# Four gated tiles and the residual rows transposed by VectorE in blocks, with the tap spectrum and the decay issued later

## The chip, the cores and the metric

One core of a Trainium2 chip runs the whole kernel. Its engines are TensorE (PE; its weight loads are listed as PEld), VectorE (DVE), ScalarE (ACT), GpSimd (POOL) and SyncE (SP); 16 DMA engines move data between device memory and the on-chip buffer. The metric is the device time of one execution in microseconds.

## The reference

Two post-norm layers over 256 latent tokens with 256 context tokens ahead of them, width 1024, in fp32. Layer 0 mixes tokens with a conformer convolution, layer 1 with a bidirectional mLSTM; each is followed by a squared-ReLU MLP.

```python
# each sub-layer: x <- LN(ALPHA*x + gate * F(x*(1+scale)+shift))
def conformer_conv(u, rows, w_pw1, b_pw1, w_dw, b_dw, ln_g, ln_b, w_pw2, b_pw2):
    a = u @ w_pw1 + b_pw1
    a = a[..., :CONV_DIM] * jax.nn.sigmoid(a[..., CONV_DIM:])
    ...
        a = dwconv(a, w_dw)                                   # 31 taps
    ...
    a = jax.nn.silu(layer_norm(a + b_dw, ln_g, ln_b))
    return a @ w_pw2 + b_pw2

def mlstm_chunk_scan(q, k, v, i_pre, f_pre, state):
    ...
    lf = jax.nn.log_sigmoid(f_pre)
    ...
        bcum = jnp.cumsum(lfc, axis=-1)
        dlog = bcum[..., :, None] - bcum[..., None, :] + ic[..., None, :]
    ...
def mlstm_features(...):
    up = u @ w_up
    ...
    q, k, v = xc @ w_q, xc @ w_k, xm @ w_v
    gates = jnp.concatenate([q, k, v], axis=-1) @ w_gate + b_gate
    o = jax.nn.sigmoid(xm @ w_o + b_o)
```

## The kernel before

**Products.** Activations lie with channels on the 128 partitions and the 512 tokens along them. An fp32 product is made of three matmuls (lines 182, 185, 186, or 213 to 215): each operand is split in a high and a low part, and low times low is dropped. For weights, SP loads a block of 1 MB into a buffer `raw` (three buffers, line 145); ACT copies each half to its high part `wh` (line 151), and DVE subtracts that from the source to get the low part `wl` (line 152). Four pairs of such parts exist. A split stands in the order of ACT and DVE among all else that these engines do.

**Order.** A tile scheduler puts the instructions of each engine in a fixed order and adds the waits; `issue_after` holds an instruction back behind another one. Each queue runs in order, so an instruction that waits holds up all that stand behind it on its engine. The DMAs have eight completion lanes in turn; a DMA can also wait for the one that used its lane before.

**Start.** The first weights are those of the adaLN unit (`ada_w`, line 344), with `start0` and its fellows loading a block of x, a block of pw1 and a block of ada_w for each of eight steps. The small parameter columns `vecs` (408 floats for each partition) come in two DMAs: 64 columns first, and the rest after the second step's loads (lines 117 and 657).

**The convolution.** `pw1_epi` gates the outputs of the first product: for tile f, ACT takes the sigmoid of the gate (line 791) and DVE multiplies (line 795). The gated tile `a` has 128 channels and 512 tokens. The convolution is done in the frequency domain over windows of tokens, so the tiles must stand with tokens on the partitions, in A (4 blocks of 128 tokens x 1024 channels). `turn` does that with four transposes on TensorE (line 806) into a PSUM bank `ln`, which ACT copies to A (line 807). Tiles 0 to 2 are kept in `turns` and turned when the next output of the product is at hand. There are two `ln` banks. `taps(h)` makes half of the spectrum of the taps: two matmuls from a table `tab` of cosines and sines (line 741), which DVE makes in some 25 small steps, each result copied by ACT to `Hc` and `Hs` (line 742). The forward products of A stand at line 830.

**The residual rows.** At the head of layer 1, x of the latent tokens, scaled for the residual, is written as token rows to device memory (`r_dr`): 16 transposes on TensorE (line 1202) with ACT's copies (line 1204) into R, one write on ACT's queue, and a load back into R (`res`) in the attention stage, where it is needed at the end of that layer. v is turned differently, by DVE in blocks of 32x32 (line 1261): the blocks' places are then put right by the write to device memory.

**The gates and the attention stage.** `gate_o` makes the output gate's product and yields after every few matmuls; other work, written as generators, is stepped forward in these places. One of them, `decay`, makes the log forget gates `lf` on ACT and DVE (ending with line 1421 on DVE), their running sums with triangular matrices on TensorE (line 1435), the columns `acol`, their transposes (line 1443) and the row maxima. A `yield` in it sets how many steps of `gate_o` go by.

Of the kernel before, what the change touches and what calls it, by code (L numbers as in the profile page):

```python
# [71 lines left out]
def hybrid_kernel(ctx: ExitStack, tc: tile.TileContext, xT, vecs_d, wdw_d, ada0_w, ada_w, wg_d, pw1a, pw1, pw2, w1_0, w2_0,  # L72
# [583 lines left out]
    start0(1)  # L656
    nc.sync.dma_start(vecs[:, NV0:], vecs_d[:, NV0:])
    for f in range(DT):
# [121 lines left out]


    A = padp.tile([P, 4, D], F32, name="A")
# [18 lines left out]
    turns = []  # L801

# [108 lines left out]
    def pw1_next(m, ps):  # L911
# [12 lines left out]
        pw1_epi(m + KO0, ps)  # L924
        if m in (1, 2):
            taps(m - 1)
        if m in (4, 6):
# [262 lines left out]

    def rows_tile():
        return xp.tile([P, 2, D], F32, tag="res", name=nm("res"), bufs=1)

    r_dr = dp.tile([P, 2, D], F32, name="r_dr")
    R = rows_tile()
    for f in range(0, DT, 2):
        t, tr = tmp("S"), psum("cv")
        for i in range(2):
            nc.scalar.activation(t[:, i * C:(i + 1) * C], x[f + i][:, HI], AF.Identity, scale=al[:, 0, f + i:f + i + 1],
                                 bias=al[:, 1, f + i:f + i + 1])  # L1200
            for tt in range(2):
                nc.tensor.transpose(tr[:, tt * C + i * P:tt * C + (i + 1) * P],
                                    t[:, i * C + tt * P:i * C + (tt + 1) * P], ident)
# [188 lines left out]
    def decay(_):  # L1392
# [36 lines left out]
        yield  # L1429
        yield  # L1430
        bps = psum("ln")
        for d, cum in ((0, upper), (1, lower)):
# [533 lines left out]
def _layout(np, i):  # L1966
    g = {k: np.asarray(v) for k, v in i.items()}
    a, turned = {}, _turned(np)
    a["xT"] = np.concatenate([g["ctx"][0], g["x"][0]], axis=0).T
    vec = {  # L1970
        "c_ctx": _cols(g["c_ctx"]), "c": _cols(g["c"][0]),
        "b_pw1": _cols(g["conv_b_pw1"][0]),
        "cln_g": _cols(g["conv_ln_g"][0]), "cln_b": _cols(g["conv_ln_b"][0]),
# [16 lines left out]
    a["wg_d"] = wg.reshape(3, ET, P, 16).transpose(0, 2, 1, 3).reshape(3, P, 256)  # L1990
    pw1 = g["conv_w_pw1"][0].reshape(D, 2, DT, P).transpose(0, 2, 1, 3)[:, :, ::-1, :].reshape(D, 2 * D)
    a["pw1a"] = pw1[:, :512].reshape(DT, P, 512)
# [14 lines left out]
    a["w2_1"] = g["mlp_w2"][1].reshape(16, 2, P, D).transpose(0, 2, 1, 3).reshape(16, P, 2048)  # L2007
    ab = g["ada_b"][1].reshape(6, D)
    a["rows_d"] = np.stack([ab[2], ab[5], g["ln1_g"][1], g["ln1_b"][1], g["ln2_g"][1], g["ln2_b"][1]])
# [24 lines left out]
```

## Time and profile before

| | |
|---|---|
| three runs | 1668.18, 1663.39, 1667.71 us; median 1667.71 |
| the profiled execution | 1665.14 us, its span 1663.4 us, granted TensorE clock 0.999 |
| busy | PE 1648.7, DVE 1038.1, ACT 734.6 us |
| DMA | 303.70 MB, 183 GB/s on average |

How to read the rows: engine, source line, operation, the tile written, an arrow, and the tiles read. In a row of the chain or the timeline the first two numbers are the start from the span's beginning and the length; what stands in square brackets is the idle time of the engine before the instruction and what ended it. "xN" counts instructions that were merged. A row of the waits gives the total, the number of times and the longest, in us. A row by stretches gives, after the stretch and its length, the busy time and number of instructions of PE, PEld, DVE, ACT and POOL, then the granted clock, the share of the DMA engines' time and GB/s.

### The profile page before, as it was taken

The page shows a single profiled execution, that of the slowest core. Times are in us where ns is not written, and L with a number is a line of the kernel's source. Part 1 is how long each engine was busy: PE and PEld are TensorE (multiplying, and loading weights), DVE is VectorE, ACT ScalarE, POOL GpSimd, SP SyncE. Part 2 cuts the span into 40 slices and gives each one's busy share as a digit, 9 for nine tenths or more (in the row PEclk, how much of TensorE's full clock was granted, in tenths as well). Part 3 has the DMA queues.
Part 4 walks back from the last instruction along what each step waited for, and adds up shares of the span by engine and source line. Part 5 has one row for each costly group of instructions (what it writes and reads, how often), then busy time and mean ns, then how long its engine had stood idle before and what let it go on. Part 6 is the DMA issues. An engine that isn't in the chain of part 4 may idle for free.

```text
span 1663.4 us, 22731 instructions
## 1 busy us (share of the span) xinstructions
PE 1648.7 (99%) x8856; PEld 1357.6 (82%) x8856; DVE 1038.1 (62%) x1863; ACT 734.6 (44%) x1182; POOL 14.4 (1%) x64
## 2 busy tenths in 40 slices
PE   9999999999999999999999999999999999999998
PEld 6665898888888998877787899888877888878886
DVE  6554895666535765762354753553489876776677
ACT  4313573232324476652233533442477654555453
POOL 0000000000000000000000000000000000000001
PEclk9999999999999999999999999999999999999999
DMA  9555223534324065557774852554465555675552
GB/s 353 208 210 214 92 75 111 167 123 148 136 101 152 4 228 194 184 196 266 278 259 146 302 179 79 179 194 144 148 240 197 203 215 203 250 284 183 178 194 85
DMA packets 74331, 303.70 MB, mean 183 GB/s; under 512 B 7694, under 2 KB 23858, under 8 KB 44144
## 3 DMA queue, kind: packets, MB, share of 16 engines
q1 hardware_dynamic: 56368, 286.49, 49.1%
q10 hardware_dynamic: 17856, 15.77, 2.8%
q8 instruction: 69, 1.13, 0.3%
q14 instruction: 38, 0.31, 0.1%
HBM read 285.42 MB, written 16.81 MB: 182 GB/s over the span
## 4 chain that ended last, share of the span: by engine, by line
PE 95%; DVE 2%; DMA 1%; ACT 1%; issue 0%; SPq 0%; DVEq 0%; ACTq 0%
PE mm L182 18%; PE mm L185 17%; PE mm L186 17%; PE mm L197 7%; PE mm L198 4%; PE mm L215 3%; PE mm L213 3%; PE mm L214 3%; PE cv L213 2%; PE cv L215 2%; PE cv L214 2%; PE fl L344 1%; PE ln L182 1%; PE cv L860 1%; PE ln L214 1%; PE ln L185 1%
## 5 line engine op out<-in xcount | busy, mean ns | idle before, releaser
L152 DVE TENSOR_TENSOR wl<-raw,wh 128x1024 fp32r<-128x1024 f32 x344 | 418.7, 1221 | 245.5 <-ACT wh L151 233.4
L151 ACT CAST wh<-raw 128x1024 fp32r<-128x1024 f32 x344 | 358.6, 1051 | 469.3 <-PE mm L185 244.4
L185 PE MATMUL mm<-u,wh 128*128 128x512 f32 (+1 forms) x808 | 291.5, 361 | 0.2 <-DVE u L604 0.2
L182 PE MATMUL mm<-u,wh 128*128 128x512 f32 (+1 forms) x680 | 243.8, 359 | 0.0
L186 PE MATMUL mm<-u,wl 128*128 128x512 f32 (+1 forms) x680 | 241.3, 355 | 0.0
L185 PEld LDWEIGHTS mm<-u,wh 128*128 128x128 f32 x808 | 152.7, 189 | 23.2 <-issue 1.0
L182 PEld LDWEIGHTS mm<-u,wh 128*128 128x128 f32 x680 | 128.4, 189 | 24.4 <-issue 6.3
L186 PEld LDWEIGHTS mm<-u,wl 128*128 128x128 f32 x680 | 128.5, 189 | 17.8
L213 PE MATMUL mm<-wh,xl 128*128 128x512 f32 x256 | 101.0, 395 | 0.7 <-DVE og L1588 0.7
L182 PE MATMUL mm<-xm,wh 128*128 128x512 f32 x256 | 101.0, 394 | 0.0
L215 PE MATMUL mm<-wl,xl 128*128 128x512 f32 x256 | 100.0, 393 | 0.0
L214 PE MATMUL mm<-wh,xl 128*128 128x512 f32 x256 | 99.9, 390 | 0.0
L186 PE MATMUL mm<-xm,wl 128*128 128x512 f32 x256 | 99.7, 389 | 0.0
L182 PE MATMUL mm<-hid,wh 128*128 128x512 f32 (+1 forms) x256 | 93.3, 364 | 0.0
L186 PE MATMUL mm<-hid,wl 128*128 128x512 f32 (+1 forms) x256 | 92.8, 363 | 0.0
L185 PE MATMUL mm<-hid,wh 128*128 128x512 f32 (+1 forms) x256 | 92.8, 363 | 0.0
L197 PE MATMUL mm<-x,wh 128*128 128x512 f32 x232 | 81.1, 398 | 0.0
L185 PE MATMUL mm<-qq,wh 128*128 128x272 f32 x256 | 73.9, 289 | 0.0
L182 PE MATMUL mm<-qq,wh 128*128 128x272 f32 x256 | 73.5, 288 | 0.0
L186 PE MATMUL mm<-qq,wl 128*128 128x272 f32 x256 | 73.5, 288 | 0.0
L197 PE MATMUL mm<-u,wh 128*128 128x512 f32 x192 | 68.6, 399 | 0.0
L1099 DVE SCALAR_TENSOR_TENSOR x<-mm,ada,x 128x256 f32<-128x256 f32 x64 | 28.5, 479 | 63.4 <-PE mm L186 63.4
(537 smaller groups left out, 3249.4 us busy)
## 6 DMA issues: line engine op xcount, KB each, us to landing
raw<-w SPq DMA_DIRECT2D x64, 1024.0 KB, 4.9
raw<-wo SPq DMA_DIRECT2D x32, 1024.0 KB, 4.9
raw<-ada_w SPq DMA_DIRECT2D x22, 1024.0 KB, 7.0
ar<-ada_w SPq DMA_DIRECT2D x80, 256.0 KB, 3.9
raw<-wv SPq DMA_DIRECT2D x16, 1024.0 KB, 8.0
raw<-wqT SPq DMA_DIRECT2D x16, 1024.0 KB, 5.7
raw<-wq SPq DMA_DIRECT2D x16, 1024.0 KB, 5.8
raw<-wk SPq DMA_DIRECT2D x16, 1024.0 KB, 5.2
```

The source lines that it names most:

```text
L151: c = nc.scalar.copy(hi, src)
L152: lastsub[0] = nc.vector.tensor_tensor(lo, src, hi.bitcast(F32), op=ALU.subtract).ins
L182: a = nc.tensor.matmul(ps, wh, xh, start=start, stop=False)
L185: nc.tensor.matmul(ps, wh, xl, start=False, stop=False)
L186: lastmm[0] = nc.tensor.matmul(ps, wl, xh, start=False, stop=stop).ins
L197: todo = [lambda s_, e_: nc.tensor.matmul(ps, wh, r[0], start=s_, stop=e_), lambda s_, e_: nc.tensor.matmul(ps[:, :n], wl, r[0][:, :n], st ...
L198: lambda s_, e_: nc.tensor.matmul(ps[:, :n], wl, r[0][:, :n], start=s_, stop=e_)]
L213: nc.tensor.matmul(ps, xh, wh, start=start, stop=False)
L214: nc.tensor.matmul(ps, xl, wh, start=False, stop=False)
L215: nc.tensor.matmul(ps, xh, wl, start=False, stop=stop)
L344: a = mark_unit[0] = nc.tensor.matmul(ps[32 * j:32 * j + 32], cs[:, kt, 14 - 2 * v:46 - 2 * v], blocks[kt], start=first and kt < 4, stop=l ...
L1099: nc.vector.scalar_tensor_tensor(res[m][:, sl_], p_, g[:, m:m + 1], res[m][:, sl_], op0=ALU.mult, op1=ALU.add)
```

## The change

Four edits. The channels are permuted in the weights' layout, so that blocks of 32x32 can be put in their place by a write; that costs nothing on the chip.

1. The parameter columns come whole in the first DMA.
2. The gated tiles 0, 1, 4 and 5 are turned by DVE (`vturn3`), two tiles to a buffer; four DMAs of ACT's queue write them to `a_dr` in pieces of 64 floats, 512 pieces each. Tiles 0 and 1 are read back into A by SP behind the load that was issued last, tiles 4 and 5 by ACT's queue at output 8. Tile 2 is still kept for `turns`, and tiles 3, 6 and 7 are turned at once, on TensorE. The two groups of the tap spectrum are issued at outputs 2 and 3 instead of 1 and 2.
3. The residual rows are turned by eight DVE transposes and written by four DMAs of SP's queue in pieces of 1 KB.
4. `decay` yields twice more ahead of the running sums, and R is loaded in a later step of `gate_o`.

```diff
-    NV0 = _OFF["ada_b1"][0]
-    nc.sync.dma_start(vecs[:, :NV0], vecs_d[:, :NV0])
+    nc.sync.dma_start(vecs, vecs_d)
...
     start0(1)
-    nc.sync.dma_start(vecs[:, NV0:], vecs_d[:, NV0:])
...
+    a_dr = [dp.tile([P, 4, 2 * P], F32, name=f"a_dr{h}") for h in range(2)]
...
-        if f < 3:
+        if f == 2:
             turns.append(lambda: turn(f, a))
+        elif f % 4 > 1:
+            turn(f, a)
         else:
-            turn(f, a)
+            vturn3(f, a)
...
+    def vturn3(f, a):
+        h, m = divmod(f, 4)
+        if m == 0:
+            three.append(rows_tile().rearrange("p a b -> p (a b)")[:, 0:8 * P].rearrange("p (t q m j) -> p t q m j", q=4, m=2, j=32))
+        vk = three[-1]
+        nc.vector.transpose(vk[:, :, :, m, :], a)
+        if m == 1:
+            for r in range(4):
+                nc.scalar.dma_start(a_dr[h][:, :, r * 64:r * 64 + 64].rearrange("(q j) t x -> j t q x", j=32),
+                                    vk[32 * r:32 * r + 32].rearrange("j t q m i -> j t q (m i)"))
+            if h == 0:
+                with tc.issue_after(loaded[0]):
+                    mark["read"] = nc.sync.dma_start(A[:, :, 0:2 * P], a_dr[0]).ins
...
-        if m in (1, 2):
-            taps(m - 1)
+        if m == 8:
+            with tc.issue_after(mark["gate"]):
+                nc.scalar.dma_start(A[:, :, 512:512 + 2 * P], a_dr[1])
+        if m in (2, 3):
+            taps(m - 2)
...
-                nc.sync.dma_start(half[i], ada_w[0, 6 + ada_s2.n, 0, :, i * 512:(i + 1) * 512])
+                with tc.issue_after(mark["read"]):
+                    nc.sync.dma_start(half[i], ada_w[0, 6 + ada_s2.n, 0, :, i * 512:(i + 1) * 512])
...
-            for tt in range(2):
-                nc.tensor.transpose(tr[:, tt * C + i * P:tt * C + (i + 1) * P],
-                                    t[:, i * C + tt * P:i * C + (tt + 1) * P], ident)
-        nc.scalar.copy(R[:, :, f * P:(f + 2) * P], tr.rearrange("p (t c) -> p t c", t=2))
-    nc.scalar.dma_start(r_dr, R)
+            nc.vector.transpose(vr[:, :, :, f + i, :], t[:, i * C:(i + 1) * C])
+    for r in range(4):
+        nc.sync.dma_start(r_dr[:, :, r * C:(r + 1) * C].rearrange("(q j) t x -> j t q x", j=32),
+                          vr[32 * r:32 * r + 32].rearrange("j t q m i -> j t q (m i)"))
...
+        yield
+        yield
         yield
         yield
         bps = psum("ln")
...
-            if (h, d) == (0, 1):
+            if (h, d) == (1, 1):
                 with tc.issue_after(loaded[0]):
                     nc.sync.dma_start(R, r_dr)
```

The scheduler makes new orders from that. ACT at the tap spectrum, before (`raw_820` is the third load of pw1, `ln_678` and `ln_681` the first tap groups, `ln_641` the bank of gated tile 1):

```order
L807 COPY A<-ln_641 128x4x128
L151 CAST wh_822<-raw_820 128x1024
L742 ACTIVATE Hc<-ln_678,pc 128x512
L742 ACTIVATE Hs<-ln_681,pc 128x512
L151 CAST wh_878<-raw_820 128x1024
L791 ACTIVATE E_722<-mm_684,vecs 128x512
L807 COPY A<-ln_716 128x4x128
```

And ACT there now (`raw_817` is the same load, `ln_707` the bank of gated tile 2):

```order
L793 ACTIVATE E_713<-mm_675,vecs 128x512
L150 CAST wh_819<-raw_817 128x1024
L150 CAST wh_875<-raw_817 128x1024
L825 COPY A<-ln_707 128x4x128
L740 ACTIVATE Hc<-ln_715,pc 128x512
L740 ACTIVATE Hs<-ln_718,pc 128x512
```

Both casts and the copy of tile 2 now come ahead of the two copies of the spectrum. TensorE in the same place now (`mm_676` is an output of pw1, `ln_707` tile 2's bank, `ln_715` and `ln_718` the tap groups):

```order
L181 MATMUL mm_676<-u_154,wh_721 128x512
L184 MATMUL mm_676<-u_155,wh_721 128x512
L824 MATMUL ln_707<-ident,E_644 128x128 x4
L739 MATMUL ln_715<-L_574,tab 128x512
L185 MATMUL mm_676<-u_154,wl_722 128x512
L181 MATMUL mm_676<-u_196,wh_721 128x512
L184 MATMUL mm_676<-u_197,wh_721 128x512
L185 MATMUL mm_676<-u_196,wl_722 128x512
L739 MATMUL ln_718<-L_574,tab 128x512
```

The transposes of tiles 0 and 1, which stood 51 matmuls ahead of this place, are gone; the second group takes the bank of tile 2, with four matmuls after the first. VectorE in the decay, before (`E_10714` becomes `lf`; the `wl` rows are weight splits of wo):

```order
L152 TENSOR_TENSOR wl_10880<-raw_10877,wh_10879 128x1024
L1417 RECIPROCAL E_10713<-E_10713 128x144
L152 TENSOR_TENSOR wl_10910<-raw_10877,wh_10909 128x1024
L1418 TENSOR_TENSOR E_10713<-E_10713 128x144
L1419 TENSOR_TENSOR E_10714<-E_10713,E_10714 128x144
L1423 MEMSET E_10713 128x144
L1421 TENSOR_TENSOR E_10714<-E_10714 128x144
```

And now, with other numbers for the same tiles (`E_10694` is `lf`):

```order
L151 TENSOR_TENSOR wl_10854<-raw_10851,wh_10853 128x1024
L1435 RECIPROCAL E_10693<-E_10693 128x144
L151 TENSOR_TENSOR wl_10876<-raw_10851,wh_10875 128x1024
L1436 TENSOR_TENSOR E_10693<-E_10693 128x144
L151 TENSOR_TENSOR wl_10918<-raw_10915,wh_10917 128x1024
L1437 TENSOR_TENSOR E_10694<-E_10693,E_10694 128x144
L1441 MEMSET E_10693 128x144
L1439 TENSOR_TENSOR E_10694<-E_10694 128x144
```

One more split, of the next load, stands between the reciprocal and the last step of `lf`.

More of the change, by code (lines that the diff above doesn't have):

```diff
@@ L779, in wgq_last, with rows_tile @@
                               qtr.rearrange("p (b j c) -> p j b c", b=4, j=4)[:, :, :, 0:16])
+    def rows_tile():
+        return xp.tile([P, 2, D], F32, tag="res", name=nm("res"), bufs=1)
     A = padp.tile([P, 4, D], F32, name="A")
+    a_dr = [dp.tile([P, 4, 2 * P], F32, name=f"a_dr{h}") for h in range(2)]
     Y = [[U() for _ in range(2)] for _ in range(4)]
@@ L1189, in hybrid_kernel @@
         pass
-    def rows_tile():
-        return xp.tile([P, 2, D], F32, tag="res", name=nm("res"), bufs=1)
     r_dr = dp.tile([P, 2, D], F32, name="r_dr")
-    R = rows_tile()
+    vr = rows_tile().rearrange("p a (b m j) -> p a b m j", m=DT, j=32)
     for f in range(0, DT, 2):
-        t, tr = tmp("S"), psum("cv")
+        t = tmp("S")
         for i in range(2):
@@ L1968, in _layout @@
     a, turned = {}, _turned(np)
-    a["xT"] = np.concatenate([g["ctx"][0], g["x"][0]], axis=0).T
+    xs = np.arange(D).reshape(4, DT, 32).transpose(1, 0, 2).reshape(D)
+    for n in ("conv_w_pw1", "mlp_w1", "ml_w_up"):
+        g[n] = np.concatenate([g[n][:1][:, xs], g[n][1:]])
+    for n in ("conv_w_pw2", "mlp_w2", "conv_b_pw2", "ln1_g", "ln1_b", "ln2_g", "ln2_b"):
+        g[n] = np.concatenate([g[n][:1][..., xs], g[n][1:]])
+    ab = g["ada_b"][1].reshape(6, D)
+    for n in ("ada_w", "ada_b"):
+        t = g[n].reshape(2, -1, 6, D)
+        g[n] = np.concatenate([t[:1][..., xs], np.concatenate([t[1:, :, :2][..., xs], t[1:, :, 2:]], axis=2)]).reshape(g[n].shape)
+    a["xT"] = np.concatenate([g["ctx"][0], g["x"][0]], axis=0).T[xs]
+    glu = np.arange(D)
+    for h in (0, 512):
+        glu[h:h + 256] = h + np.arange(256).reshape(4, 2, 32).transpose(1, 0, 2).reshape(256)
     vec = {
         "c_ctx": _cols(g["c_ctx"]), "c": _cols(g["c"][0]),
-        "b_pw1": _cols(g["conv_b_pw1"][0]),
+        "b_pw1": _cols(g["conv_b_pw1"][0].reshape(2, D)[:, glu].reshape(-1)),
         "cln_g": _cols(g["conv_ln_g"][0]), "cln_b": _cols(g["conv_ln_b"][0]),
@@ L1990, in _layout @@
     a["wg_d"] = wg.reshape(3, ET, P, 16).transpose(0, 2, 1, 3).reshape(3, P, 256)
-    pw1 = g["conv_w_pw1"][0].reshape(D, 2, DT, P).transpose(0, 2, 1, 3)[:, :, ::-1, :].reshape(D, 2 * D)
+    pw1 = g["conv_w_pw1"][0].reshape(D, 2, D)[:, :, glu].reshape(D, 2, DT, P).transpose(0, 2, 1, 3)[:, :, ::-1, :].reshape(D, 2 * D)
     a["pw1a"] = pw1[:, :512].reshape(DT, P, 512)
```

3 lines of the change are left out of this document (1 added, 2 removed).

## The prediction

> **What bounds the kernel now.** I read the page first, then the waits of TensorE, then the chain of waits, then the timeline around each place that the change touches.
>
> ```profile
> span 1663.4 us, 22731 instructions
> PE 1648.7 (99%) x8856; PEld 1357.6 (82%) x8856; DVE 1038.1 (62%) x1863; ACT 734.6 (44%) x1182; POOL 14.4 (1%) x64
> PE 95%; DVE 2%; DMA 1%; ACT 1%; issue 0%; SPq 0%; DVEq 0%; ACTq 0%
> ...
> PE ln L1435 <- DVE E L1421: 1.6, 1, 1.6
> PE fl L344 <- DMA raw<-ada_w: 1.4, 2, 1.2
> PE cv L176 <- DVE ones L130: 1.1, 1, 1.1
> PE mm L213 <- DVE og L1588: 0.7, 1, 0.7
> PE ln L741 <- issue: 0.6, 1, 0.6
> ```
>
> TensorE is busy for 1648.7 of 1663.4 us and carries 95% of the chain that ends last. So an instruction taken from it is worth its place in the queue. All its waits together are a few us, and the change touches four of the five largest. DVE (62%) and ACT (44%) have room on average; whether they have it where they are asked is the question.
>
> **What leaves TensorE.** The chain of waits has the removed transposes as pieces of its own (start, length, what):
>
> ```profile
> 50.68 0.87 PE ln L806 x8
> 57.24 0.58 issue
> 57.82 1.95 PE ln L741 x4
> ...
> 101.39 0.59 PE ln L806 x4
> ...
> 120.12 0.44 PE ln L806 x4
> ...
> 629.23 0.87 PE cv L1202 x8
> ```
>
> Gated tiles 0 and 1 are the first x8, tile 4 is at 101.39, tile 5 at 120.12: 0.87 + 0.59 + 0.44 = 1.90 us. The residual rows have 16 transposes. Eight stand at 629.23 and cost 0.87; the other eight are strung between matmuls, where each also breaks the stream:
>
> ```profile
> 632.23 0.39 PE L185 MATMUL mm<-u,wh 128*128 128x512 f32 x1
> 632.47 0.38 PE L1202 MATMUL cv<-ident,S 128*128 128x128 f32 x2
> ...
> 634.28 0.40 PE L182 MATMUL mm<-u,wh 128*128 128x512 f32 x1
> ...
> 51.62 0.40 PE L185 MATMUL mm<-u,wh 128*128 128x512 f32 x1
> ...
> 56.85 0.39 PE L182 MATMUL mm<-u,wh 128*128 128x512 f32 x1
> ```
>
> From 51.62 to 56.85 there are 23 starts: a pitch of 0.227 us. From 632.23 to 634.28 there are five pitches, 1.14 us undisturbed; 2.05 were taken, so 0.91. Together 1.78 us.
>
> DVE does the same work with other instructions: four of 128x512 and eight of 128x256.
>
> ```profile
> L1261 DVE STREAM_TRANSPOSE res<-vt 128x512 f32<-128x512 f32 x16 | 11.3, 707 | 31.0 <-ACT vt L1248 31.0
> 620.00:640.00 20.00, 20.00 (x134) 18.25 (x134) 7.45 (x9) 13.21 (x23) 0.00 (x0) 1.00 0.77 289
> ```
>
> At 0.7 us each the four cost 2.8 us of DVE; half the size I put at 0.4 (estimate from that row, 0.35 to 0.7), 3.2 us for eight. Around 630 DVE is busy 7.45 of 20 us (third figure), so the residual rows are covered; ACT even loses four copies. Their write now stands on SP's queue ahead of the fourth up_x load, but three loads are already out in front of it. I count nothing for it; if the cover failed, the price would be one load's lateness there, 1 to 2 us.
>
> **The tap groups an output later.** Before, TensorE stood 0.58 us at 57.24 for a table that DVE finished just then. Moved some 5.5 us later (24 pitches), the groups find it ready: -0.58. The 1.95 us of matmuls only move.
>
> **The new wait in the same place.** ACT's order changes there: now two casts of the third pw1 load and the copy of tile 2 stand ahead of Hc and Hs, and the second tap group needs the bank that the copy frees. Those casts wait for a load that is late already:
>
> ```profile
> 50.86 0.36 SPq L145 DMA_DIRECT2D raw<-pw  x1
> 61.35 1.05 ACT L151 CAST wh<-raw 128x1024 fp32r<-128x1024 f32 x1 [8.98 <-DMA raw<-pw]
> 51.00:57.00 6.00, 6.00 (x31) 4.91 (x28) 5.83 (x17) 1.37 (x3) 1.97 (x8) 1.00 1.00 374
> 57.00:61.00 4.00, 3.42 (x12) 1.74 (x11) 1.34 (x3) 0.00 (x0) 0.03 (x1) 1.00 0.13 48
> 75.84 0.70 PE L830 MATMUL mm<-A,ge 128*128 128x512 f32 x1
> ```
>
> Issued at 50.86, it lands at 61.3. Until 57 all DMA engines are busy (1.00, 374 GB/s); then at 0.13 one or two of them work off a rest. Now 512 KB in 2048 pieces of 256 bytes go into that same stretch. The nearest row for small pieces is the window 760 to 930 us, where the row of the write queue stands for pieces of some 500 bytes, and the start of the kernel, where the parameter columns are read in 128 pieces of 256 bytes:
>
> ```profile
> q10 hardware_dynamic: 8448, 4.20, 8.7%
> 2.00:3.00 1.00, 1.00 (x7) 1.00 (x7) 0.00 (x0) 0.97 (x5) 1.00 (x6) 1.00 0.66 82
> 5.00:7.00 2.00, 0.82 (x11) 0.66 (x13) 0.00 (x0) 0.71 (x4) 0.00 (x0) 1.00 1.00 396
> ```
>
> 8.7% of 16 engines over 170 us, by 8448, is 28 ns a piece. Half as long a piece lies between 14 and 28 ns: 2048 of them are 1.8 to 3.6 us of all 16 engines. I take 2.7, because a write of the same kind is the nearer row. The landing goes to 64.0, and the copy is done two casts and a copy later (1.05 + 1.05 + 0.55), at 66.6. TensorE reaches the second group after 51 pitches from 50.5, the transposes of tile 2 (0.44), the first group (half of 1.95), four more pitches and an adaLN matmul (0.1): 50.5 + 11.6 + 0.4 + 1.0 + 0.9 + 0.1 = 64.6. So it waits 2.0 us. The lower end is 0.3 (a gate activation ahead of the casts ends at 62.3 even if the load is early), the upper 3.8 (3.6 us, and DVE's transposes push the issue by some tenths).
>
> [...]
>
> The read back into A is needed at 75.84 by the forward products. It is issued when the writes have landed; even at 64 it has 11 us for 512 KB. SP has nothing due before 65.8 behind it. Tiles 4 and 5 come back after 131 and are needed at 145: hidden.
>
> **The first load.** 344 more columns (176 KB) now stand ahead of the first two weight loads.
>
> ```profile
> 2.67 7.83 DMA raw<-ada_w
> 10.63 1.07 PE L344 MATMUL fl<-raw,cs 128*32 128x256 f32 x16 [0.24 <-DMA raw<-ada_w]
> ```
>
> At 396 GB/s (row 5 to 7 above) they take 0.44 us; TensorE already waits for the second load at 10.63, so a later landing counts in full. The small pieces that they replace moved only 82 GB/s, so some comes back: +0.35, from 0.2 to 0.5.
>
> **Decay later.** TensorE stands longest for the running sums of the decay:
>
> ```profile
> 1214.39 0.39 PE L214 MATMUL mm<-wh,xl 128*128 128x512 f32 x1
> 1216.40 0.49 PE L1435 MATMUL ln<-E,tri 128*128 128x128 f32 x2 [1.63 <-DVE E L1421]
> ...
> 1214.25 1.19 DVE L152 TENSOR_TENSOR wl<-raw,wh 128x1024 fp32r<-128x1024 f32 x1
> 1216.08 0.27 DVE L1421 TENSOR_TENSOR E<-E 128x144 f32<-128x144 f32 x1
> ...
> 1214.41 1.05 ACT L151 CAST wh<-raw 128x1024 fp32r<-128x1024 f32 x1 [0.22 <-DMA raw<-wo]
> 1193.00:1232.00 39.00, 37.34 (x171) 29.03 (x167) 27.55 (x60) 26.17 (x42) 1.31 (x3) 1.00 0.72 250
> 1232.00:1262.00 30.00, 29.32 (x130) 23.06 (x129) 28.93 (x69) 26.63 (x50) 0.00 (x0) 1.00 0.55 186
> ```
>
> In the new order five more matmuls stand ahead of the sums: TensorE arrives 5 x 0.227 = 1.1 us later. But DVE now does one more weight split (1.19) ahead of the last two steps of the same values, and that split needs the cast of a load which landed at 1214.4 before. So the values come about 1.2 us later too: the wait stays, 0 in the sum, from -1.6 (it goes) to +1. After it, the transposes of the columns have eight instead of four matmuls' time. The wait of 0.7 for og (L1588) should go: og stands earlier in DVE's order against the splits, and its bank is asked for two matmuls later. I count -0.7, from 0 to -0.7.
>
> **Sum.** -1.90 - 1.78 - 0.58 - 0.70 + 0.35 + 2.0 + 0 = -2.6 us. The profiled execution took 1665.14 us, so 1662.5. The median shown is 1667.71, of runs from 1663.39 to 1668.18; the profiled one lies low among them, so against the median the forecast looks larger than it is. About 0.3% (5 us) is what a measurement of this kernel tells from no change, and the forecast lies right at that bound below the median.
>
> **The rivals.**
> (a) *The new wait in front of the second tap group does not come.* For it: DMA at 57 to 61 is nearly idle (0.13), so if the rest in that stretch belongs to the two loads of 31 rows on one or two engines and pw1's share is elsewhere, the small writes fit into the gap. Against: the casts waited to 61.35 in just that stretch. Sum -4.6 + 0.3: 1660.8.
> (b) *Decay later pays.* The extra split is ready early, because the 1 MB of the residual rows no longer stands ahead of that load; the wait for the sums goes: 1662.5 - 1.6 = 1660.9. Against: the split still takes its 1.19 us on DVE.
> (c) *The small pieces cost like the parameter columns; this one ends slower than before.* In 2 to 3 us the engines were busy 0.66 x 16 = 10.6 us; 49 of the 82 KB at 396 GB/s are 2.0 of it, so 128 pieces took 8.6, 67 ns each. Then 2048 pieces are 8.6 us of all engines, the load lands at 69.9, the copy is done at 72.5, and TensorE waits 7.9 us: -4.6 + 7.9 = +3.3, 1668.4. It decides from 44 ns a piece on (5.6 us), where the wait eats the whole 4.6. Against: the start has first latencies in it, and v's writes at 28 ns are the same kind.
> [...]
> (d) *DVE falls behind in the attention stage.* It is busy 28.93 of 30 us at 1232 to 1262. If the decay work pushed back by about two splits (2.4 us) is not absorbed, less 1.07 idle, and the same lateness returns at each of four heads' outputs, TensorE waits 4 x 2.4 - 1.1 = 8.5 us: 1671. Against: DVE is busy 27.55 of the 39 us before, so it enters the stage with room.
> (e) *The decay change does nothing*: that is the forecast's own value for it, 0.
>
> **How the numbers follow.** Forecast 0.42, (a) 0.22, (b) 0.10, (c) 0.16, (d) 0.10. The forecast's own bounds come from its three open terms (the tap wait -1.7 to +1.8, the sums -1.6 to +1, og +0.7), which will hardly all fall on one side: 1660 to 1665. For 8 in 10 the range reaches over (a) and (b) below, with their bounds, and over (c) above: 1658.0 to 1668.5; it leaves out (d) and the far end of (c). Faster by over 0.3% (below 1662.7): half of the forecast, most of (a) and (b), 0.45. Within: the rest of these and most of (c), 0.42. Slower (above 1672.7): most of (d) and the far end of (c), 0.13.
>
> **What would show it.** Right: no transposes beyond tiles 2, 3, 6, 7 on TensorE and none at 630; no wait for the tap table; a wait of about 2 us at the second tap group with ACT's copy as the releaser, and the third pw1 cast starting near 64; a wait of about 1.6 for the running sums; og's wait gone. Wrong: no wait at the tap group and the cast at 61 (rival a), or that cast at 67 and later (c); DVE as releaser of TensorE again and again after 1230 (d).

## The result, and the profile after

| | before | after |
|---|---|---|
| median | 1666.49 us (1663.39 to 1668.18, 6 runs) | 1660.64 us (1659.72 to 1662.42, 6 runs) |
| profiled execution (span) | 1665.14 us (1663.4) | 1660.27 us (1658.5) |

The changed kernel takes 0.9970 of the time before, with an interval of 0.9959 to 0.9982. The forecast was 1662.5 us with a range of 1658.0 to 1668.5. The two profiled executions differ by 4.9 us where the sum said 2.6, so most terms have to be looked at one by one.

The page of the changed kernel, and the waits of TensorE (total, times, longest, in us):

```profile
span 1658.5 us, 22680 instructions
PE 1646.7 (99%) x8824; PEld 1355.1 (82%) x8824; DVE 1042.1 (63%) x1875; ACT 730.4 (44%) x1174; POOL 14.3 (1%) x64
...
PE cv L175 <- DVE ones L129: 1.1, 1, 1.1
PE fl L343 <- DMA raw<-ada_w: 1.0, 2, 0.6
PE mm L212 <- ACT wh L150: 0.8, 1, 0.8
PE ln L1455 <- DVE E L1439: 0.3, 1, 0.3
```

TensorE has 32 instructions fewer (16 of the gated tiles, 16 of the residual rows). The tap table's wait and og's wait are gone, the running sums' wait fell from 1.6 to 0.3 (L1435 is now L1455), and a wait of 0.8 for a weight part (L212) is new. The new wait that the forecast priced at 2.0 us, for the second tap group, is not in the list.

**Where the time went, in order.** The chain of waits has the same adaLN products (`fl`) as marks in both kernels; the shift of their starts shows how far ahead TensorE is. Before (start, length, what):

```profile
73.28 0.99 PE fl L344 x8
...
90.92 1.85 PE fl L344 x16
...
111.46 1.85 PE fl L344 x16
...
141.68 1.85 PE fl L344 x16
```

After:

```profile
10.29 1.07 PE fl L343 x16
...
61.04 0.98 PE fl L343 x2
...
63.11 1.05 PE ln L739 x2
65.29 1.05 PE ln L739 x2
70.65 0.99 PE fl L343 x6
...
90.37 1.85 PE fl L343 x16
...
110.33 1.85 PE fl L343 x16
...
140.11 1.85 PE fl L343 x16
```

The first load comes 0.34 us earlier (10.63 to 10.29). At 90 the lead is 0.55 us, after tile 4 it is 1.13, and after tile 5 1.57. So tiles 4 and 5 gave what their transposes cost, 0.58 and 0.44. Tiles 0 and 1 and the tap wait should have given 0.87 + 0.58 before 90 and gave almost nothing. Two rows say why. The adaLN group at 61 stands in two pieces: two instructions for 0.98 us, and six more at 70.65 for 0.99, where before eight took 0.99 (73.28). And the tap groups, which were one piece of four for 1.95, are two of 1.05.

At the residual rows the same instructions of TensorE shift from 1.56 us ahead at 620 to 3.36 at 640: a gain of 1.80 where 1.78 was forecast. DVE is then 12.28 of 20 us busy, against 7.45 before, and TensorE waits nowhere:

```profile
620.00:640.00 20.00, 20.00 (x119) 17.84 (x119) 12.28 (x16) 11.24 (x18) 0.14 (x2) 1.00 0.79 257
```

At the running sums the lead goes from 3.09 us at 1212 to 5.36 at 1300, and at 1409 the new wait takes about 1.2 back: 4.10 at 1420, 4.23 at 1650. The landing of the last write is another 0.7 earlier.

**Why the tap wait did not come.** SP's queue, ACT's part and the DMA queues of 46 to 62 us, after:

```profile
40.04 0.32 SPq L733 DMA_DIRECT2D L<-wdw_d  x1
51.07 0.34 SPq L144 DMA_DIRECT2D raw<-pw  x1
61.08 0.69 ACT L793 ACTIVATE E<-mm,vecs 128x512 f32<-128x512 f32 x1 [9.82 <-PE mm L185]
61.66 1.98 ACT L150 CAST wh<-raw 128x1024 fp32r<-128x1024 f32 x2
63.55 0.59 ACT L825 COPY A<-ln 128x512 f32<-128x512 f32 x1
q10 hardware_dynamic: 2112, 0.52, 14.0%
raw<-pw SPq DMA_DIRECT2D x1, 1024.0 KB, 8.4
```

The pw1 load was issued at 51.07 and landed 8.4 us later, at 59.5. Before it took until 61.3 without any small pieces in its way; the forecast had 64.0. The casts start at 61.66 behind the gate's activation, the copy is done at 64.1, and the second tap group starts at 65.29 without a wait. One part of what had made the load late before stands in the first row: one of the two loads of the taps (`L`, 31 rows, 62 KB) moved to 40.04, more than 10 us ahead of the pw1 load. Before, both were issued just ahead of it:

```profile
48.97 0.63 SPq L735 DMA_DIRECT2D L<-wdw_d  x2
51.26 0.90 SPq L939 DMA_DIRECT2D S<-ada_w  x2
```

The second row is another part, which the prediction passed over. Before, two loads of 256 KB (`S<-ada_w`) went out right behind the pw1 load; the change holds them back behind the read of `a_dr`:

```profile
60.73 1.08 SPq L961 DMA_DIRECT2D S<-ada_w  x2
```

So the 512 KB of small pieces came into the stretch as 512 KB of other loads left it. No run here separates the two parts.

The pieces' price can be read too: 14.0% of 16 engines over 16 us, by 2112 packets, is 17.0 ns for each of 256 bytes. The forecast took 21 (2.7 us for 2048), between 14 and 28.

**The decay.** The load ahead of the sums (`raw<-wo`), ACT's cast behind it, and TensorE's sums; before and after:

```profile
1200.24 0.33 SPq L145 DMA_DIRECT2D raw<-wo  x1
1207.03 2.00 ACT L151 CAST wh<-raw 128x1024 fp32r<-128x1024 f32 x2 [3.21 <-DMA raw<-wo]
```

```profile
1197.14 4.21 SPq L144 DMA_DIRECT2D raw<-wo  x2
1202.02 2.00 ACT L150 CAST wh<-raw 128x1024 fp32r<-128x1024 f32 x2 [1.30 <-DMA raw<-wo]
1213.09 0.49 PE L1455 MATMUL ln<-E,tri 128*128 128x128 f32 x2 [0.27 <-DVE E L1439]
```

From its issue to its cast the load took 6.8 us before and 4.9 after (a row with x2 merges two loads; the first is meant), and the wait fell by 1.36. Two hundred microseconds on, a load of the same kind is the other way round. Before, the one issued at 1407.64 was cast at 1412.61, 5.0 later; after, the one at 1402.40 was cast at 1408.54, and TensorE waits:

```profile
1407.64 0.33 SPq L145 DMA_DIRECT2D raw<-wo  x1
1412.61 1.05 ACT L151 CAST wh<-raw 128x1024 fp32r<-128x1024 f32 x1 [0.93 <-DMA raw<-wo]
```

```profile
1402.40 4.87 SPq L144 DMA_DIRECT2D raw<-wo  x2
1408.54 2.00 ACT L150 CAST wh<-raw 128x1024 fp32r<-128x1024 f32 x2 [2.10 <-DMA raw<-wo]
1409.64 0.50 PE L212 MATMUL mm<-wh,xl 128*128 128x512 f32 x1 [0.76 <-ACT wh L150]
```

In both late cases the DMA queues of that stretch list one packet more than the loads, on queue 8, and the kind "instruction" says that it is a fetch of code. The first row is of before, 1200.2 to 1207.1, the second of after, 1402.4 to 1408.6:

```profile
q8 instruction: 1, 0.02, 0.9%
```

```profile
q8 instruction: 1, 0.02, 1.0%
```

The packet starts 0.52 us behind the issue of the load in the first case (1200.76) and 2.7 us behind it in the second (1405.1). The experiments below take up these three questions: the split of the adaLN group, what makes a load late in the convolution, and what the fetch does to loads.

### The profile page after: what moved, and what is told of

Its sections match the earlier page's. It is cut to its first block, busy times and chain, and to the rows that moved or that the text cites. A ratio compares the mean times of both kernels' runs of the same rounds, so it can differ in the third digit from the quotient of the medians.

```text
span 1658.5 us, 22680 instructions
## 1 busy us (share of the span) xinstructions
PE 1646.7 (99%) x8824; PEld 1355.1 (82%) x8824; DVE 1042.1 (63%) x1875; ACT 730.4 (44%) x1174; POOL 14.3 (1%) x64
## 3 DMA queue, kind: packets, MB, share of 16 engines
q8 instruction: 69, 1.13, 0.3%
## 4 chain that ended last, share of the span: by engine, by line
PE 96%; DVE 2%; DMA 1%; ACT 1%; issue 0%; SPq 0%; DVEq 0%; ACTq 0%
PE mm L181 18%; PE mm L184 17%; PE mm L185 17%; PE mm L196 7%; PE mm L212 4%; PE mm L197 4%; PE mm L214 4%; PE mm L213 4%; PE fl L343 2%; PE cv L212 2%; PE cv L214 1%; PE cv L213 1%; PE ln L181 1%; PE cv L878 1%; PE ln L184 1%; PE fl L765 1%
## 5 line engine op out<-in xcount | busy, mean ns | idle before, releaser
L212 PE MATMUL mm<-wh,xl 128*128 128x512 f32 x256 | 101.1, 395 | 0.8 <-ACT wh L150 0.8
L1121 DVE SCALAR_TENSOR_TENSOR x<-mm,ada,x 128x256 f32<-128x256 f32 x64 | 28.5, 479 | 61.3 <-PE mm L185 61.3
```

The costliest lines, as they stand in the source:

```text
L212: nc.tensor.matmul(ps, xh, wh, start=start, stop=False)
L1121: nc.vector.scalar_tensor_tensor(res[m][:, sl_], p_, g[:, m:m + 1], res[m][:, sl_], op0=ALU.mult, op1=ALU.add)
```

## The experiments

**The adaLN group whole** (from the changed kernel).

```diff
-            ada_g1.mm(first, range(4))
+            with tc.issue_after(lastmm[0]):
+                ada_g1.mm(first, range(4))
```

> The changed kernel, with the adaLN group of four matmuls in the convolution (first half of the gate unit) held behind the last matmul of output 3, so that the scheduler doesn't send one of the four ahead. Theory S (the four fill four column tiles of TensorE at once, so one alone costs as much as four: in the changed kernel one alone took 0.98 us and the other three 0.99): the two pieces become one of about 1.0, the span falls by 0.9 to 1.0 us, to about 1657.5. Theory T (the single one filled a stall or replaced work that comes later): the piece of 0.98 goes and a wait of the same size appears in front of the tap groups, the span stays at 1658.5.

Median 1658.82 us (1658.48 to 1660.1, 5 runs), 0.9962 of before, interval 0.9948 to 0.9977. The intervals of this and of the change overlap, so the size is read from the trace. In the chain the group is one piece again (the second row is the next group):

```profile
69.66 1.00 PE fl L343 x8
...
71.25 0.99 PE fl L343 x8
```

From 45 to 95 us TensorE gains 1.37 us on the changed kernel. So the split of the group had taken at least its piece of 0.98 us from what the removed transposes gave; the other 0.4 us came with the new order around it and is not assigned to a row.

**The tap groups back at outputs 1 and 2** (from the changed kernel).

```diff
-        if m in (2, 3):
-            taps(m - 2)
+        if m in (1, 2):
+            taps(m - 1)
```

> The changed kernel, with the tap spectrum's groups at outputs 1 and 2 again. Theory S: the later place split the adaLN group, so here the group is whole again (one piece of 1.0 instead of 0.98 and 0.99), and the wait for the tap table of before comes back (0.58, perhaps 1.0 since the table is some tenths later): sum between -0.4 and 0. Theory T (the later place is a gain of 0.58, as the prediction had it): 0.6 us slower in this stage.

1660.06 us, one run, so only its trace is used (span 1658.3). The wait for the table is back, and still the stretch from 45 to 95 is 1.06 us shorter than in the changed kernel, since here the scheduler leaves the adaLN group whole:

```profile
PE ln L739 <- DVE tab L713: 0.5, 1, 0.5
```

The later tap groups do remove their wait of 0.5 to 0.6; in the schedule that came of it they cost about 1.1 us more than they save.

**The parameter columns in two loads again** (from the changed kernel).

```diff
-    nc.sync.dma_start(vecs, vecs_d)
+    nc.sync.dma_start(vecs[:, :NV0], vecs_d[:, :NV0])
...
+    nc.sync.dma_start(vecs[:, NV0:], vecs_d[:, NV0:])
```

> The changed kernel, with the parameter columns loaded in two DMAs again (64 columns first). Theory P (the prediction's term: 176 KB more ahead of the first weights cost 0.35 us): TensorE's first two adaLN pieces start 0.2 to 0.5 us earlier than 6.46 and 10.29. Theory Q (the small first DMA costs more than its bytes, and its second one more still): they start 0.3 to 0.5 us later, near the 6.89 and 10.63 of before. Theory N (it is the variation of one run to the next): either, without order.

1660.11 us (one run), span 1658.4. At 10 us TensorE is 0.08 us earlier than in the changed kernel. Six other kernels with the one load and the same start lie from 0.20 earlier to 0.27 later there, so the 0.35 of the forecast lies within what the start varies by from run to run, and nothing of it is seen.

**The small pieces doubled** (from the changed kernel): each of the four writes of tiles 0 and 1 goes out a second time, into a buffer that nobody reads.

```diff
+            for r in range(4 if h == 0 else 0):
+                nc.scalar.dma_start(a_two[:, :, r * 64:r * 64 + 64]..., vk[32 * r:32 * r + 32]...)
```

> The changed kernel, with tiles 0 and 1 written twice (four more DMAs of 512 pieces of 256 bytes, to another tensor). By the 17 ns a piece that the trace of the changed kernel gives (14.0% of 16 engines over 16 us by 2112 pieces), 2048 more pieces are 2.2 us of all engines: the third load of pw1 lands at about 61.6 instead of 59.5, just when ACT comes to it (61.66), and TensorE's wait at the second tap group is 0 to 0.3 us. If a piece costs 28 ns, as the prediction's upper bound: landing 63.1, wait about 1.5 us. If the write queue's pieces don't delay the loads at all: landing 59.5.

1662.07 us (one run), span 1660.4. The queue's row of 46 to 66 us, ACT's issue, the gate's activation behind it, and the one wait that it made:

```profile
q10 hardware_dynamic: 4224, 1.05, 22.5%
raw<-pw SPq DMA_DIRECT2D x1, 1024.0 KB, 8.9
50.80 9.28 ACTq L819 DMA_DIRECT2D a_dr<-res  x4
60.13 0.69 ACT L794 ACTIVATE E<-mm,vecs 128x512 f32<-128x512 f32 x1 [12.25 <-DMA a_dr<-res]
PE ln L828 <- DVE E L798: 0.9, 1, 0.9
```

22.5% of 16 engines over 20 us by 4224 is 17.0 ns again. Twice the pieces moved the pw1 load's landing by only half a microsecond (8.4 to 8.9 from issue). But the pieces did not all go out at once: the second four issues held ACT's queue for 9.28 us, and a DMA of `a_dr` ended the 12.25 us that ACT stood before the activation, so this run says less of the load than it was meant to. The cost came from the queue that stood still: the gate's activation behind it started only at 60.13, and TensorE waited 0.9 us for that tile. The scheduler again left the adaLN group whole here, which pays for that wait, so that the stretch from 45 to 95 took as long as in the changed kernel; of the 1.8 us by which the span is longer, 0.3 had arisen ahead of it and the rest arose later, in places that the edit does not touch.

**The tap loads first, in the kernel before.** The two 31-row loads are issued ahead of `bdw`.

```diff
+    wds = [tmp("L")[:NTAP, :] for _ in range(2)]
+    for h_ in range(2):
+        nc.sync.dma_start(wds[h_], wdw_d[0:NTAP, h_ * 512:(h_ + 1) * 512])
+
     bdw = padp.tile([P, D], F32, name="bdw")
...
-    wds = [tmp("L")[:NTAP, :] for _ in range(2)]
-    for h_ in range(2):
-        nc.sync.dma_start(wds[h_], wdw_d[0:NTAP, h_ * 512:(h_ + 1) * 512])
```

> The kernel before, with the two loads of 31 tap rows issued ahead of the adaLN load and of the bias row instead of behind (the changed kernel's scheduler had sent one of them ahead). In the trace of the changed kernel one such load alone in flight moved 26 GB/s, one DMA engine's rate. Theory S (one engine has 62 KB more to do for each of them, 2.4 us, and the third load of pw1 ends when that engine does): with both out before the loads begin to crowd, that load lands 2 to 4.8 us earlier than 61.3, at 57 to 59, though its issue is unchanged. Theory T (its landing is set by all engines together): it lands at 61 as before.

1666.87 us (one run). The cast of the third pw1 load starts at 58.79; it was 61.35 before:

```profile
58.79 1.05 ACT L151 CAST wh<-raw 128x1024 fp32r<-128x1024 f32 x1 [6.71 <-DMA raw<-pw]
```

So the two loads of 31 rows just ahead of it had held it up by 2.6 us, without a single small piece beside it. They went out at 39.79, and `bdw`, which was ahead of them, now stands in their place at 48.70 with more bytes than they had; the two `S` loads behind the pw1 load are as before. The time rose because of another place: the wait for the running sums was 1.93 us and the granted clock fell behind it. Two stretches of this kernel (the clock is the figure after POOL's; before had 1.00 in both):

```profile
1215.00:1220.00 5.00, 3.07 (x13) 2.56 (x13) 3.70 (x14) 1.12 (x2) 0.00 (x0) 0.80 0.89 338
1220.00:1225.00 5.00, 5.00 (x22) 3.84 (x21) 4.01 (x6) 2.07 (x3) 0.00 (x0) 0.86 0.04 18
```

In finer stretches the clock was 0.50 for 3.4 us, from 1218.0, 1 us after the end of the wait. TensorE lost 1.95 us against before between 1212 and 1300, 0.3 of them by the longer wait.

**The decay's edits, one at a time.** Three kernels: the changed one with R loaded as before, the changed one without its two yields, and the kernel before with R loaded late.

```diff
-            if (h, d) == (1, 1):
+            if (h, d) == (0, 1):
```

> The changed kernel, with the residual rows loaded back in the early step of the output gate again (1 MB ahead of the third load of wo), the two later yields kept. Theory S (it is the load's place, not the yields, that let the wait for the running sums go: without 1 MB ahead the weight load lands earlier and the split in front of the last steps is ready): the wait comes back, 1.0 to 1.8 us instead of 0.27, and the stage from 1190 to 1300 us loses 1.3 to 2.3 us. Theory T (the yields did it): the wait stays at 0.3.

```diff
-        yield
-        yield
```

> The changed kernel, without the two added yields. The running sums stand in the same place of TensorE's order, only the transposes of the row maxima come 12 matmuls earlier. Theory S: the wait for the running sums stays at 0.3 and the stage's time within 0.3 us. Theory T (the yields did it): the wait comes back to 1.6 and the stage loses 1.3 us or more.

```diff
-            if (h, d) == (0, 1):
+            if (h, d) == (1, 1):
```

> The kernel before, with nothing changed but the place of the residual rows' load (in the later step of the output gate). Theory S: the wait for the running sums falls from 1.63 to about 0.3, and the wait for og (0.67) goes or stays small: the stage from 1190 to 1300 us gains 1.3 to 2.3 us. Theory T: no change of the wait.

They took 1661.35, 1660.97 and 1664.54 us, one run each. Neither undoing brought the sums' wait back: it is in neither trace, and the stretch from 1212 to 1300 is 0.8 and 0.6 us longer than in the changed kernel (for R early, with a wait of 0.76 for a weight part). In the third kernel the wait was 0.32 us, so R's load looked like the cause there; the next kernel contradicts that. That kernel also had a dip of the clock at the tap table: 2.5 us after the end of a wait of 0.60 us (0.58 before), behind the four tap matmuls, the clock was 0.50 for 3.4 us, its matmuls stood 0.43 us apart from 59.8 to 63.2 instead of 0.227, and it lost 1.6 us (first row; the second is before):

```profile
60.00:70.00 10.00, 10.00 (x35) 6.89 (x35) 2.45 (x2) 5.68 (x8) 0.00 (x0) 0.84 0.43 140
```

```profile
60.00:70.00 10.00, 10.00 (x42) 7.06 (x41) 2.45 (x2) 5.68 (x8) 0.00 (x0) 1.00 0.42 138
```

Of the fourteen traces two show a dip, both of 3.4 us at 0.50 and both within 2.5 us behind a wait (0.60 and 1.93 us); waits of 0.58 to 1.76 us in the other traces were followed by nothing.

**The kernel before without its waits**: tap groups late, tap loads first, R late, and nothing else of the change.

```diff
-        if m in (1, 2):
-            taps(m - 1)
+        if m in (2, 3):
+            taps(m - 2)
...
-            if (h, d) == (0, 1):
+            if (h, d) == (1, 1):
```

> The kernel before with its 48 transposes on TensorE, but without its two waits: tap groups an output later, tap rows loaded first, residual rows loaded in the later step of the output gate. Theory S (a wait of TensorE of 0.6 us or more is at times followed by some us at a lower granted clock, which costs 1.6 to 2 us more than the wait; in single looks one followed the tap wait and one the wait for the running sums): without the waits every run has a mean clock of 0.998 to 0.999, and the median falls by more than the waits themselves (0.6 + 1.3 us): by 2.5 to 4, to 1661.5 to 1663, with a spread under 2 us. Theory T (the clock goes down by itself): the clocks and the spread stay as before (0.996 to 0.999, 5 us), the median falls by 1.9 to about 1663.8.

Median 1663.55 us (10 runs; one at 5832 us was disturbed, the other nine lie from 1661.07 to 1665.81 with a median of 1663.25), 0.9985 of before, interval 0.9976 to 0.9995. The tap wait is gone, but the sums' wait stands with R late:

```profile
PE ln L1435 <- DVE E L1421: 1.8, 1, 1.8
```

So R's place does not decide it, and as a test of the clock this kernel fails, since one of the waits stayed in. In its trace a code fetch starts at 1199.9 us, 0.66 us behind the issue of the load of that place, which took 7.0 us to land. In the kernel with R late alone the fetch started at 1201.7, 0.35 us behind the issue, the load took 5.5 us, and the wait was 0.32.

**The fetch moved.** The queue of the fetches, by the page of before and of after alike (packets, MB, share):

```profile
q8 instruction: 69, 1.13, 0.3%
```

That is a packet of 16 KB for every 24 us on average. I take them to be TensorE's code, the longest by far (8824 matmuls and as many weight loads of 22680 instructions in the changed kernel); no row names the engine. If a packet delays the load beside it, a few more instructions at the start must move the packet against the work. Twelve more idle products, 24 matmuls in the trace, go in at the start (beside the whole adaLN group).

```diff
-    idle(spare, 5)
+    idle(spare, 17)
```

> The kernel with the adaLN group held whole, with twelve more idle products at the start (24 matmuls in the trace, some 3 us, which compute nothing that is used). Nothing else is changed, but TensorE's instruction stream is 24 matmuls with their weight loads longer ahead of all that follows, so the fetches of its code, one packet of 16 KB about every 29 us on one DMA engine, come 24 x 0.227 = 5.4 us earlier against the work. Theory F (a load that has such a fetch in its stretch lands about 1.2 us later: without one the load in front of the running sums landed 4.8 to 4.9 us after its issue, with one 5.6 to 6.8): the fetch that stood at 1204.0 in the kernel with the group held whole comes into the load in front of the running sums (1196.1 to 1200.9 there), and the one at 1404.0 leaves the load of 1401.6 to 1407.8. So the wait for the running sums comes back (0.8 to 1.9 us, from none), and the wait of 1.0 for the cast of that later load goes. Theory N (the landing depends on the kernel's tensors or on chance): none for the sums, 1.0 for the cast, as it was. Besides, if a long wait of TensorE is at times followed by a lower clock: with the wait for the sums back, some runs have a mean clock of 0.997 or 0.998 and lie 1.5 to 2 us above the others; else all have 0.999.

Median 1661.57 us (10 runs), 0.9982 of before, interval 0.9972 to 0.9991: the start is 2.2 us later, which is the price of the added products. The stretches tell the rest. The fetch stands at 1401.2 instead of 1404.4, off the late `wo` load, which now takes 4.9 us (issued 1404.14) instead of 6.2; TensorE's wait of about 1 us there is gone, and it gains 1.33 us between 1402 and 1420 on the kernel with the group whole. (Near 1245 two waits of 0.5 and 0.4 us came that this kernel's parent did not have; I have no cause for them.)

```profile
1404.14 4.88 SPq L144 DMA_DIRECT2D raw<-wo  x2
...
1409.04 1.05 ACT L150 CAST wh<-raw 128x1024 fp32r<-128x1024 f32 x1 [0.86 <-DMA raw<-wo]
```

The other half of the expectation failed: the fetch was also to fall on the sums' load and bring that wait back. It fell at 1202.5, in the last half microsecond of a load that ran from 1198.14 to 1202.9, and no wait came.

**Two more tiles on DVE, and the fetch moved the other way.** The first of these turns tiles 2 and 6 by DVE as well, written by SP in pieces of 128 bytes and read back (with the adaLN group whole). The second is the same with six idle products (12 matmuls) fewer at the start.

```diff
+        if f in (2, 6):
+            vturn1(f, a)
...
+        nc.vector.transpose(vk, a)
+        for r in range(4):
+            nc.sync.dma_start(o_dr[h][:, :, r * 32:r * 32 + 32]..., vk[32 * r:32 * r + 32]...)
+        nc.sync.dma_start(A[:, :, f * P:(f + 1) * P], o_dr[h])
```

> The kernel with the adaLN group held whole, and tiles 2 and 6 turned by DVE as well, each written alone (2048 pieces of 128 bytes) and read back, by SP's queue. Theory S (an instruction taken from TensorE is worth its place, if the tile is back in time): two pieces of 0.44 to 0.5 us less, about 1657.8. Against it: tile 2 is gated at 58.9 and needed at 72; its write (1.5 to 2.5 us of all engines, four issues), and its read behind the other tiles' read, must be done in 13 us; if it comes later, each us counts in full on TensorE, and the kernel is slower than 1658.8. Theory T (the DMAs push the loads behind them on SP's queue, as tile 2's writes stand ahead of an adaLN load): a new wait of 0.5 us or more at the adaLN groups or at the forward products.

```diff
-    idle(spare, 13)
+    idle(spare, 7)
```

> The kernel with the adaLN group held whole and tiles 2 and 6 by DVE, with six idle products fewer at its very start, where TensorE waits for the first load anyway (12 matmuls of the trace). The code fetch that stood at 1403.0, in the stretch of the wo load issued at 1399.3 (landed at 1405.7, 6.4 us), comes 12 x 0.227 = 2.7 us later, to 1405.7. Theory F: that load lands 4.9 us after its issue, TensorE's wait of 1.0 for its cast goes, and the kernel takes about 1657.2; the fetch at 1202.5 goes to 1205.2, into the next load, whose cast is not waited for by more than some tenths. Theory N: the wait stays, 1658.2. If the missing idle products leave the clock lower at the start, the first adaLN pieces take longer than 1.0 us each.

The first has a median of 1658.25 us (6 runs), 0.9962 of before, interval 0.9950 to 0.9975; its lead on the kernel with the whole group grows by 0.3 at tile 2 and 0.5 at tile 6. Its wait at the late load was 1.03 us. The second has a median of **1656.65 us** (1656.64 to 1658.68, 4 runs), 0.9956 of before, interval 0.9940 to 0.9973, the least of all here. Its late load took 5.0 us (issued 1399.89, cast at 1404.87), no wait follows, and TensorE gains 1.38 us on the first of the two between 1400 and 1420:

```profile
span 1654.9 us, 22657 instructions
...
1399.89 4.88 SPq L144 DMA_DIRECT2D raw<-wo  x2
...
1404.87 1.05 ACT L150 CAST wh<-raw 128x1024 fp32r<-128x1024 f32 x1 [0.95 <-DMA raw<-wo]
```

But the fetch moved less than expected: from 1403.5 to 1404.2, not to 1405.7. Since the load was issued 0.6 us later too, the fetch starts 4.30 us behind the issue instead of 4.15. That it was forced off the load is shown by the kernel with the twelve added products alone; here it stands 0.5 us ahead of the landing and did no harm.

The fourteen traces can be read together. At the late `wo` load eight kernels have a fetch that starts 2.0 to 4.15 us behind the issue: the load takes 6.0 to 6.3 us, and TensorE waits 0.76 to 1.05. The other six have none, or one at 4.3: the load takes 4.8 to 4.9, and TensorE does not wait. And of all the 1 MB loads during which almost nothing else moved (0.05 MB at most), 463 had no fetch and took 4.6 to 5.4 us; of 30 with a fetch that started in their first 4 us, 12 took more than that, up to 7.4. Of 105 with a later fetch three did. So a fetch can delay a load, but not every fetch does, and one near the load's end hardly ever does.

## Why the prediction was right, and where it was not

The measured time lies in the range, and the median came out as the forecast's "faster" (below 1662.7). That the number is so near is in part luck, because misses cancelled. In the profiled executions the tap wait that did not come (2.0), the sums' wait (1.36) and the start (0.7) made the kernel faster than forecast, the tap groups with the split adaLN group (1.1) and a new wait at 1409 (1.2) made it slower. Step by step:

- **What leaves TensorE** held where it could be read alone: tile 4 0.58 (said 0.59), tile 5 0.44 (0.44), the residual rows 1.80 (1.78). The 0.87 of tiles 0 and 1 left TensorE too, but their stage gave it back: the step "the 1.95 us of matmuls only move" was wrong. The groups cost 2.10 apart, and the adaLN group beside them was split by the scheduler, 0.98 more. The kernel with the group whole shows that second term. No step of the prediction looked at how TensorE's own order changes at 61 us.
- **The tap wait gone**: right, 0.58. The kernel with the groups early has it again (0.5).
- **The new wait of 2.0** failed: it is 0. The term mis-sized was the landing, put at 64.0 and measured at 59.5. The prediction had taken the late landing of before as given and added to it. But the tap loads ahead had made it late, 2.6 us for both as the kernel before with these loads first shows, and the new order had moved one of them away; and 512 KB of adaLN loads beside it, held back by the change itself, left the stretch as the pieces came. How much each of the two gave in the changed kernel is open. The price for a piece was 17.0 ns where 21 was used, a smaller miss. (The upper end of 3.8 does not follow from its terms either: with 3.6 us for the pieces the same sum gives a wait of 2.9 and some tenths.) So rival (a) is what happened, in part for the reason that it gave, the loads of 31 rows.
- **Rival (c)**, 67 ns for a piece, is refuted: 17.0 ns, twice.
- **The first load, +0.35**: nothing seen; the step "a later landing counts in full" was right only within a start that varies by more.
- **The running sums, 0**: failed, it was -1.36. Rival (b) named the right end and blamed the residual rows' 1 MB ahead of the load; the runs do not bear this out (with R late the wait was 0.32 in one kernel and 1.76 in another). The waits of 1.63, 1.76 and 1.93 go with loads that have a code fetch 0.52 to 0.66 us behind their issue and took 6.7 to 7.05 us to land; with the fetch 0.35 us behind it the load took 5.5 and the wait was 0.32; in the changed kernel the fetch came after the load, at 1205.5, the load took 4.8, and the wait was 0.27. At the late `wo` load that tie was forced by moving the fetch; at this load it was not, so here it is argued and not shown.
- **og, -0.7**: right in the changed kernel; of its variants some show 0.3 to 0.4.
- **DVE behind in attention**, rival (d): refuted; no such waits, and the lead at 1330 (5.36) is that at 1300 (5.36). Its own time, 1671, also lies below the 1672.7 from which the chances counted it as slower.
- **Unforeseen**: the wait of 0.8 at 1409, some 1.2 us of lead, from a code fetch on a load; with 32 matmuls and their weight loads gone from TensorE, the fetches stand at other places of the work than before (1405.1 us here, 1401.1 before).

The trace's gain in the profiled executions was 4.9 us and that of the medians 5.85. What may fill the rest is the clock: of 44 executions of the kernel before beside these experiments, 17 had a mean granted clock of 0.997 or less; of 31 of the changed kernel and of four variants without the two waits, none. That the waits bring the dips fits the two places found, within 2.5 us behind a tap wait and a sums' wait; but no kernel here forced it, and it stays open.

## What to carry to other kernels

Before adding to a load that is late, ask what made it late: a narrow transfer ahead of it can make it late while most DMA engines stand idle (here two loads of 62 KB held 1 MB up by 2.6 us, and from 57 to 61 us 0.13 of the engines were busy), and moving that can be worth more than its bytes suggest. Count also what the edit takes out of the stretch, not only what it adds. When work is taken from the engine that bounds, look for what the scheduler puts into the gap, above all small groups whose matmuls start together (of the adaLN group two took 0.98 us, and all eight 0.99). And when a wait of a microsecond comes or goes at a place that was not touched, look at the instruction fetches beside the loads (here 1 MB took 6.0 to 6.3 us with one, and 4.8 to 4.9 without) as well as for a reason in the edit.

## What the runs showed of the hardware

- At the late `wo` load, 1 MB took 6.0 to 6.3 us to land where a code packet of 16 KB started 2.0 to 4.15 us behind its issue, and 4.8 to 4.9 without one or with one later. Twelve added products moved the packet away and gave TensorE 1.33 us; with six products fewer it started 0.15 us later in the load, and 1.38 us came back. Of 30 loads of 1 MB with a packet in their first 4 us and almost nothing else beside them, 12 took more than the 5.4 us that 463 without one took at most. In the changed kernel's list above no wait of TensorE is put down to code; what it paid at that place was the wait of 0.76 us for the late load.
- Pieces of 256 bytes, written to device memory, cost 17.0 ns of one DMA engine each, whether there were 2112 or 4224.
- Two loads of 31 rows, 62 KB each, delayed the 1 MB load behind them by 2.6 us. In the changed kernel one such load, alone in flight from 47.2 to 48.0, kept 0.07 of the 16 engines busy, about one of them, and moved 26 GB/s.
- A group of adaLN matmuls in a 32-column form costs 0.98 us with two of its instructions sent alone, 0.99 with six and 0.99 with all eight: its price does not follow the number.
- The clock fell to 0.50 for 3.4 us, once 1 us behind a wait of 1.93 us and once 2.5 us behind one of 0.60, at about 1.6 us each; other traces have such waits without it.
